# First columns of a modulation summed half on TensorE, deeper weight look-ahead in the mixer, and stage edges that keep their last weight blocks (hybrid macaron layer, Trainium2)

## The chip, the core and the metric

The kernel runs on one core of one Trainium2 chip. The metric is the device time of one execution in microseconds (us); lower is better. The kernel before took 2037.12 us, the median of three runs between 2032.08 and 2038.51 us.

## What is computed

One decoder layer on 256 tokens with a model width of 2048, all in float32. A condition vector `c` gives nine modulation vectors (shift, scale and gate of three parts). A SwiGLU network (FFN1, inner width 5632), a token mixer and a second SwiGLU network (FFN2) each read a normalised and modulated `x` and add their gated result to it:

```python
cond = silu(c)
mod = cond @ ada_w + ada_b                       # 2048 -> 9 * 2048
sh1, sc1, gt1, sh2, sc2, gt2, sh3, sc3, gt3 = split(mod, 9)
h = rmsnorm(x, g0) * (1 + sc1) + sh1
x = x + 0.5 * gt1 * ((silu(h @ w_gate1) * (h @ w_up1)) @ w_down1)
h = rmsnorm(x, g1) * (1 + sc2) + sh2
x = x + gt2 * (concat(forgetting_attention(h), gated_delta_rule(h)) @ w_out)
h = rmsnorm(x, g2) * (1 + sc3) + sh3
x = x + 0.5 * gt3 * ((silu(h @ w_gate2) * (h @ w_up2)) @ w_down2)
return rmsnorm(x, final_norm)
```

The mixer has eight attention heads with a forget gate and eight heads of a gated delta rule in chunks of 64 tokens; the latter needs a causal convolution of its inputs and the inverse of small triangular matrices.

## The kernel before

**Weights.** All large weights (353 MB, 5392 tiles) stream through once in a fixed list of blocks. A block is eight 128x128 tiles, 512 KB. `Stream.block` (L98) issues its DMA from SyncE (SP) into `wraw` (L103) and a ScalarE (ACT) cast to the reduced type, `whi` (L106); `Stream.low` (L109) has VectorE (DVE) write what the cast lost, `wlo` (L113). `wraw`, `whi` and `wlo` have three buffers each, and in some stages a fourth set for every fourth block. TensorE (PE) multiplies high by high, low by high and high by low (L576, L577, L579 in `products`). A *step* is four tiles against both halves of the tokens, six matmuls with 512 columns; two steps use up a block. In the mixer's input projections (`mm`, L516) a tile costs one matmul with 512 columns (L517) and one with 256 (L518).

**Order.** The program is emitted in order, and a scheduler fixes one instruction list per engine. Each engine works its list strictly in order, so a waiting instruction holds all behind it. `Stream.next` (L126) emits a block's load, cast and subtraction when its first tile is asked for; blocks in `W.early` (the mixer's) are emitted by `ahead` while the block before them is used, one block ahead. `tc.issue_after` pins an instruction behind another.

**Modulation.** Each of the 144 columns of `mod` needs 128 sums over 2048 numbers: a 1 MB load into a place of pool `adap` and one DVE reduction over 128x2048 (`ada_sum`, L286; two halves for the first two columns, L762). The table `RATE` says how many columns are emitted per block from a block number on; `W.quiet` stops them. The first 32 are the scale and shift columns of FFN1, two per `k`, since FFN1 needs `hs[k]`, its modulated input for `k` (128 of the 2048), `k` by `k`.

**Start.** `c` is loaded as a row (`crow`), spread to 128 partitions by matmuls (`pcs`, L226), passed through silu into `cs`; column 0 is loaded ahead of `x`; all squares of `x` are ACT's (L752), and DVE turns their sum into the row norm (`fv`, L771, to `frb`, L777). PE makes the transposes of `x` and some dummy matmuls (`warm_up`, L218). FFN1 then runs `k` in chunks 0-2, 2-8, 8-16 (`CHUNKS`); at the start of a chunk four groups of gate and up columns are run side by side for some `k` (`pgu`), afterwards one after the other. ACT copies the sums of chunk 0 to `acc` (L614).

**Edges.** The normalisation needs whole rows of `x`, so at the end of FFN1, of the mixer's output projection and of FFN2, `last_block` (L665) does the last ten steps for the first 128 tokens first and then for the others, so that the residual of the first half (`rs`, L540, `x`, L541), its square sum (`jq`, L384) and its inverse root (`nstd`, L396 to L401) are done meanwhile. The last six of these steps run first, and their weights are loaded a second time for the second half: three blocks per edge. Of the next stage, `modulate` (L425) transposes `xn` into `pxt` (L439) and scales it into `hs` (L451, L452) for `k` 0 and 1 of the first tokens ahead of the edge; that covers two `k` of the next stage for these tokens (12 matmuls `pv`, L857 to L859, in the mixer), until the second half's `xn` is there.

**Mixer.** Between the projections lie chains of small operations of the heads, cut into pieces by `tick` and `advance`. SP's list also holds the small DMAs of the triangular solve (`ld`, L1027; `x<-ld`, L1032; `xi<-x`, L1047), which wait for DVE.

## Time and profile before

| | |
|---|---|
| median of three runs | 2037.12 us |
| the profiled execution's own time | 2035.86 us |
| its span, first to last instruction | 2034.1 us |
| mean granted clock of PE | 0.991 |
| PE busy | 1987.4 us, 98% |
| DVE busy | 1494.7 us, 73% |
| ACT busy | 1001.4 us, 49% |
| moved by DMA | 528.92 MB, mean 260 GB/s |

A profile row of the timeline gives start, duration, engine, line of the kernel, what is written from what, the count, and in brackets the idle time of the engine before it with what ended it. A row of the waits gives who waited for whom, the sum, the count and the longest. Matmuls are pipelined: the time from the start of one to the start of the next is what counts, not a row's duration. FFN1 takes the span to about 771 us, the mixer to 1284 us, FFN2 to the end.

### The profile page before, as it was taken

To read this page: it belongs to the slowest core of one execution; us is meant where nothing else is said; L and a number is where in the kernel's file an instruction comes from. 1 tells how busy PE (TensorE), PEld (TensorE's weight loads), DVE (VectorE), ACT (ScalarE), POOL (GpSimd) and SP (SyncE) were. 2 spreads that over 40 slices of the span, in tenths; PEclk is the share of its full clock that TensorE was granted. 3 is DMA by queue.
4 is the path that set the end of the run, shared out by engine and by line. 5 is a ranking of instruction groups with operands and counts; after the bars stand their busy time and mean duration, and the time that the engine had idled before them with its cause. 6 is when DMAs were issued, how large, how long until landed. Compare 5 with 4: busy or idle time off the path is not lost.

```text
span 2034.1 us, 25528 instructions
## 1 busy us (share of the span) xinstructions
PE 1987.4 (98%) x9385; PEld 1648.0 (81%) x9385; DVE 1494.7 (73%) x2096; ACT 1001.4 (49%) x1451; POOL 2.6 (0%) x15
## 2 busy tenths in 40 slices
PE   8999999999999999998999999999999999999998
PEld 5788888888888887887888888788888888888886
DVE  6899999898787886689877887765566565455455
ACT  5544444343433456685657655644444333444444
POOL 0000000000000000000000000000000000000000
PEclk8999999999999999999999999999999999999999
DMA  8989898999788886564656577666666665555554
GB/s 323 349 326 349 314 344 333 354 387 375 298 331 338 325 304 243 185 214 155 209 205 220 187 259 267 219 218 239 249 243 231 239 238 196 187 192 189 207 195 167
DMA packets 134511, 528.92 MB, mean 260 GB/s; under 512 B 18489, under 2 KB 23785, under 8 KB 116081
## 3 DMA queue, kind: packets, MB, share of 16 engines
q1 hardware_dynamic: 134386, 527.29, 71.2%
q8 instruction: 73, 1.20, 0.2%
q14 instruction: 52, 0.43, 0.1%
HBM read 521.82 MB, written 5.41 MB: 259 GB/s over the span
## 4 chain that ended last, share of the span: by engine, by line
PE 91%; DVE 3%; DMA 3%; ACT 2%; issue 1%; ACTq 0%; DVEq 0%; SPq 0%
PE pgu L579 15%; PE pgu L577 15%; PE pgu L576 15%; PE pd L577 8%; PE pd L576 8%; PE pd L579 8%; PE pp L517 6%; PE pp L518 3%; DMA wraw<-in_w_dram 2%; DVE wlo L113 2%; PE pv L857 1%; PE pv L859 1%; PE pv L858 1%; PE po L577 1%; PE po L576 1%; PE po L579 1%
## 5 line engine op out<-in xcount | busy, mean ns | idle before, releaser
L106 ACT CAST whi<-wraw 128x1024 fp32r<-128x1024 f32 x683 | 714.8, 1051 | 833.7 <-PE pgu L577 280.3
L113 DVE TENSOR_TENSOR wlo<-wraw,whi 128x1024 fp32r<-128x1024 f32 x683 | 826.3, 1222 | 385.9 <-ACT whi L106 382.8
L576 PE MATMUL pgu<-whi,hs 128*128 128x512 f32 x1408 | 552.1, 394 | 14.8 <-ACT hs L411 6.5
L577 PE MATMUL pgu<-whi,hs 128*128 128x512 f32 x1408 | 550.5, 392 | 0.3
L579 PE MATMUL pgu<-wlo,hs 128*128 128x512 f32 x1408 | 438.0, 391 | 1.2 <-DVE wlo L113 1.2
L286 DVE CUSTOM_DVE_ANT_0 adat<-adat,cs,colt 128x2048 f32<-128x2048 f32 x140 | 328.7, 2348 | 41.4 <-DMA adat<-in_ada_dram 40.6
L576 PEld LDWEIGHTS pgu<-whi,hs 128*128 128x128 f32 x1408 | 266.0, 189 | 73.4 <-ACT hs L411 7.4
L579 PEld LDWEIGHTS pgu<-wlo,hs 128*128 128x128 f32 x1408 | 265.1, 189 | 58.4 <-DVE wlo L113 3.2
L577 PEld LDWEIGHTS pgu<-whi,hs 128*128 128x128 f32 x1408 | 266.2, 189 | 56.6 <-DVE hs L453 1.1
L576 PE MATMUL pd<-whi,hid 128*128 128x512 f32 x704 | 274.7, 390 | 0.0
L577 PE MATMUL pd<-whi,hid 128*128 128x512 f32 x704 | 273.9, 389 | 0.0
L517 PE MATMUL pp<-hs,whi 128*128 128x512 f32 x656 | 242.3, 405 | 8.7 <-ACT whi L106 8.7
L579 PE MATMUL pd<-wlo,hid 128*128 128x512 f32 x704 | 220.0, 389 | 0.0
L518 PE MATMUL pp<-hs,wlo 128*128 128x256 f32 x656 | 189.7, 290 | 1.3 <-DVE wlo L113 1.3
L576 PEld LDWEIGHTS pd<-whi,hid 128*128 128x128 f32 x704 | 132.2, 188 | 27.7 <-issue 0.2
L579 PEld LDWEIGHTS pd<-wlo,hid 128*128 128x128 f32 x704 | 132.2, 188 | 27.5
L577 PEld LDWEIGHTS pd<-whi,hid 128*128 128x128 f32 x704 | 132.2, 188 | 27.1
L517 PEld LDWEIGHTS pp<-hs,whi 128*128 128x128 f32 x656 | 124.8, 190 | 32.1 <-ACT whi L106 9.9
L518 PEld LDWEIGHTS pp<-hs,wlo 128*128 128x128 f32 x656 | 125.5, 191 | 2.5 <-DVE wlo L113 1.9
L857 PE MATMUL pv<-whi,hs 128*128 128x512 f32 x128 | 52.3, 411 | 0.5 <-ACT whi L106 0.3
L859 PE MATMUL pv<-wlo,hs 128*128 128x512 f32 x128 | 50.8, 398 | 0.0
L858 PE MATMUL pv<-whi,hs 128*128 128x512 f32 x128 | 50.6, 395 | 0.0
(313 smaller groups left out, 1369.9 us busy)
## 6 DMA issues: line engine op xcount, KB each, us to landing
wraw<-in_w_dram SPq DMA_DIRECT2D x683, 512.0 KB, 4.4
adat<-in_ada_dram SPq DMA_DIRECT2D x140, 1024.0 KB, 7.6
gtr<-gd SPq DMA_DIRECT2D x12, 256.0 KB, 6.2
rw<-rowd SPq DMA_DIRECT2D x24, 128.0 KB, 3.8
adaf<-in_ada_dram SPq DMA_DIRECT2D x4, 512.0 KB, 10.0
x<-in_xr_dram SPq DMA_DIRECT2D x4, 512.0 KB
adaf<-in_ada_dram SPq DMA_DIRECT2D x2, 1024.0 KB
xd<-x SPq DMA_DIRECT2D x4, 512.0 KB
```

Source lines behind the costliest of these rows:

```text
L106: self.cast = self.nc.scalar.copy(self.h, r).ins
L113: self.sub = self.nc.vector.tensor_tensor(self.l, r, self.h.bitcast(F32), ALU.subtract).ins
L286: V.tensor_tensor_reduce(t, t, cs, HALF.get(m, 1.0), L("adab", q, 1), ALU.mult, ALU.add, mod[:, q : q + 1])
L517: PE.matmul(ps, wt[0], act.rearrange("p a t -> p (a t)"), start=first, stop=False)
L518: PE.matmul(ps[:, :T], wt[1], act[:, 0], start=False, stop=last)
L576: PE.matmul(ps[t], hi_(t), wh, start=first, stop=False)
L577: PE.matmul(ps[t], lo_(t), wh, start=False, stop=False)
L579: PE.matmul(ps[t], hi_(t), wl, start=False, stop=last)
L857: PE.matmul(pv[m][t], hs[:, k, 0, sl], wh, start=(k == 0), stop=False)
L858: PE.matmul(pv[m][t], hs[:, k, 1, sl], wh, start=False, stop=False)
L859: PE.matmul(pv[m][t], hs[:, k, 0, sl], wl, start=False, stop=(k == KD - 1))
```

## The change

**Start.** `c` is loaded as a column, passed through silu (16 columns) and spread by DVE into diagonal tiles `dg`, which four float32 matmuls with a matrix of ones turn into `pcs`. `x` is loaded ahead of the columns; two of its four square sums go to DVE. The host packs the first four columns (two pairs) so that one 1 MB tile of a pair holds half of both columns for PE and the other tile holds the other half for DVE. `pe_sums` runs eight float32 matmuls 128x256 per pair into `pm`; `pair_sums` sums the other half on DVE (128x1024 per column) and takes the diagonal of `pm` with a 128x128 reduction per column. In chunk 0 three groups run side by side, not four. The first two rows `xn` are made before the columns. Columns 4 and 5 are loaded into places of the `hid` pool; `RATE` gives no column for blocks 0 to 2, one per block for 3 and 4.

**Stream.** `load` issues a DMA apart from `block`. For the mixer's blocks in `W.early`, the load is emitted three blocks ahead, cast and subtraction two.

**Edges.** `last_block` keeps the weights of all ten steps: six in tiles `hold`, four in `whi`, `wlo`. Nothing is loaded twice (nine blocks fewer in all). The next stage's first blocks are emitted during the last steps. `modulate` does `k` 0 to 3 of the first tokens ahead of the edge; the next stage starts with 18 matmuls `pv` (mixer) or eight steps of three matmuls (FFN2) on them. `W.quiet` is set in the output projection's column block 2, and `RATE` gives more columns from block 338 on.

On PE at the start of FFN1, before (`px` transposes of `x`, `pgu` the gate and up sums):

```order
L778 MATMUL nrow<-colt,frb 128x128 x2
L784 MATMUL px<-colt,x 128x128 x8
L576 MATMUL pgu<-whi,hs 128x512 x3
L577 MATMUL pgu<-whi,hs 128x512 x3
L576 MATMUL pgu<-whi,hs 128x512
L577 MATMUL pgu<-whi,hs 128x512
L579 MATMUL pgu<-wlo,hs 128x512 x4
L576 MATMUL pgu<-whi,hs 128x512
L577 MATMUL pgu<-whi,hs 128x512
```

and after:

```order
L614 MATMUL pgu<-whi,hs 128x512 x2
L615 MATMUL pgu<-whi,hs 128x512 x2
L614 MATMUL pgu<-whi,hs 128x512
L617 MATMUL pgu<-wlo,hs 128x512 x2
L615 MATMUL pgu<-whi,hs 128x512
L614 MATMUL pgu<-whi,hs 128x512
L615 MATMUL pgu<-whi,hs 128x512
L617 MATMUL pgu<-wlo,hs 128x512 x2
L839 MATMUL pm<-adat,cstt 128x256 x8
L614 MATMUL pgu<-whi,hs 128x512
```

The sums of the second pair of columns now stand in PE's list after the first twelve `pgu` matmuls.

On ACT at the same place, before (`acc` copies of chunk 0's sums):

```order
L106 CAST whi<-wraw 128x1024 x2
L410 ACTIVATE ht<-ht,mod 128x256
L411 CAST hs<-ht 128x256
L614 COPY acc<-pgu 128x512 x2
L106 CAST whi<-wraw 128x1024
L614 COPY acc<-pgu 128x512 x2
L106 CAST whi<-wraw 128x1024
L614 COPY acc<-pgu 128x512 x4
L106 CAST whi<-wraw 128x1024
```

and after:

```order
L126 CAST whi<-wraw 128x512 x2
L427 ACTIVATE hs<-xn,mod,g_277 128x256
L126 CAST whi<-wraw 128x1024 x2
L427 ACTIVATE hs<-xn,mod,g_343 128x256
L126 CAST whi<-wraw 128x1024
L652 COPY acc<-pgu 128x512 x8
L126 CAST whi<-wraw 128x1024 x3
L652 COPY acc<-pgu 128x512
```

Eight copies of `acc` now stand ahead of the cast of the fifth block; before, casts and copies alternated.

On DVE at the edge from the mixer to FFN2, before (`rs`, `x` the second half's residual, `adat` a column, `g` the scale that `hs` needs):

```order
L401 SCALAR_TENSOR_TENSOR nstd<-nya,nstd 128x1
L286 ISA adat,mod<-adat,cs,colt 128x2048
L286 ISA mod 128x1
L113 TENSOR_TENSOR wlo<-wraw,whi 128x1024
L286 ISA adat,mod<-adat,cs,colt 128x2048
L286 ISA mod 128x1
L540 TENSOR_TENSOR rs<-po,gtr 128x512
L422 SCALAR_TENSOR_TENSOR g_11397<-mod,colt 128x16
L541 TENSOR_TENSOR x<-x,rs 128x512
L452 TENSOR_SCALAR ht<-pxt,g_11397,mod 128x128
```

and after:

```order
L416 SCALAR_TENSOR_TENSOR nstd<-nya,nstd 128x1
L134 TENSOR_TENSOR wlo<-wraw,whi 128x1024 x2
L480 TENSOR_SCALAR ht<-pxt,g_11426,mod 128x128
L481 TENSOR_TENSOR hs<-ht,hs 128x128
L480 TENSOR_SCALAR ht<-pxt,g_11426,mod 128x128
L578 TENSOR_TENSOR rs<-po,gtr 128x512
L481 TENSOR_TENSOR hs<-ht,hs 128x128 x3
L579 TENSOR_TENSOR x<-x,rs 128x512
```

The two columns are gone from there, and the first tokens' `hs` work stands ahead of the second half's residual.

The core of the diff:

```diff
-RATE = ((0, 0.5), (24, 0.34), (56, 0.45), (68, 0.35), (112, 0.45), (168, 0.38), (266, 0.4), (282, 0.0), (300, 0.17), (412, 0.125))
+RATE = ((0, 0.0), (3, 1.0), (5, 0.5), (24, 0.34), (56, 0.45), (68, 0.35), (112, 0.45), (168, 0.38), (266, 0.4), (282, 0.0), (300, 0.17), (338, 0.25), (412, 0.125))
...
-N_WARM = (10, 5)
+N_WARM = (8, 6)
...
+    def load(self, b):
+
+        more = self.more and self.home is None and b % 4 == self.odd
+        r = (self.more[0] if more else self.raw).tile([P, WB * P], F32, name="wraw")
+        for q in self.pieces(b):
+            self.last = self.nc.sync.dma_start(r[:, q], self.w[b][:, q]).ins
+        return r, more
+
+    def pieces(self, b):
+
+        n = WB * P // 2
+        return (slice(0, n), slice(n, 2 * n)) if b == 0 else (slice(0, 2 * n),)
...
             self.now = b
-            if b + 1 in self.early:
-                self.ahead(b + 1)
+            if b + 3 in self.early:
+                self.loaded[b + 3] = self.load(b + 3)
+            for a in (b + 1, b + 2):
+                if a in self.early and a not in self.ready:
+                    self.ahead(a)
...
-                    n = 4 if len(chunks) > 1 else 3
+                    n = 4 if ci else 3
                     pb = {e: (psn(2 * i, "pgu"), psn(2 * i + 1, "pgu")) for i, e in enumerate(grp[:n])}
-                first = S_IN if need is h_need and pb else 0
-                wts = {(k, e): one(pb[e], *e, k, k0, k1, (0,)) for k in range(k0, k0 + first) for e in pb}
+                ahead = [(k, e) for k in range(k0, ks) for e in pb]
+                n = 8 if hq["todo"] else 0
+                wts = {(k, e): one(pb[e], *e, k, k0, k1, (0,)) for k, e in ahead[:n]}
                 for (k, e), wt in wts.items():
                     one(pb[e], *e, k, k0, k1, (1,), wt)
-                for k in range(k0 + first, ks):
-                    for e in pb:
-                        one(pb[e], *e, k, k0, k1)
+                for k, e in ahead[n:]:
+                    one(pb[e], *e, k, k0, k1)
...
-    def last_block(steps, weights, one, ps, m_gt, squares, begin):
-
-        twice, held = steps[-S_OUT : S_AGAIN - S_OUT], steps[S_AGAIN - S_OUT :]
+    def last_block(steps, weights, one, ps, m_gt, squares, begin, home):
+
         for f in steps[:-S_OUT]:
             one(f, weights(f), (0, 1), False)
-        for f in twice:
-            one(f, weights(f), (0,), False)
-        held = [(f, weights(f)) for f in held]
-        for f, wt in held:
-            one(f, wt, (0,), f == steps[-1])
+        W.home = home
+        held = []
+        for f in steps[-S_OUT:]:
+            if len(held) == S_HOME:
+                W.home = None
+            held.append((f, weights(f)))
+            one(f, held[-1][1], (0,), f == steps[-1])
+        held = held[S_HOME:] + held[:S_HOME]
         assert len(W.order) % WB == 0 and not W.ready
         b = len(W.order) // WB
-        n = S_AGAIN * 4 // WB
-        W.ahead(b)
+        if begin:
+            W.more, W.odd = None, (b + 3) % 4
+            W.ahead(b)
         residual(ps[0], 0, 3, m_gt, squares)
-        for i in range(1, n):
-            W.ahead(b + i)
-        for f, wt in held:
-            one(f, wt, (1,), False)
-        if squares != "final":
-            W.held = [yins[0]]
-            W.ahead(b + n, roots[0])
-        for f in twice:
-            if f == twice[-2] and begin:
+        W.held = [yins[0]]
+        for n, (f, wt) in enumerate(held):
+            if begin and n == 2:
+                W.ahead(b + 1, roots[0])
+            if begin and n == 4:
+                W.ahead(b + 2)
+            if begin and n == S_OUT - 2:
                 modulate(*begin)
-                hq["todo"].pop(0)[2]()
-            one(f, weights(f), (1,), f == twice[-1])
+                for _ in range(begin[-1]):
+                    h_pop()
+            one(f, wt, (1,), n == S_OUT - 1)
         residual(ps[1], 1, 3, m_gt, squares, yins[0])
-        if squares != "final":
-            W.held = [sums[1], yins[1]]
-
...
-    hold = None
-    for kind, i in (("c", 0), ("c", 1), ("c", 2), ("c", 3), ("x", 0), ("x", 1), ("x", 2), ("x", 3)):
...
-                t, q = divmod(i, 2)
-                hold = A.activation(junk, X(t, halves[q].start, D // 2), AF.Square, accum_out=s0[:, t, q : q + 1]).ins
+    bc_ = lambda a_, q, n: a_[:, q : q + n].unsqueeze(2).to_broadcast([P, n, P])
+    pcs = []
+    for q in range(4):
+        spread = V.tensor_tensor(dg[:, 4 * q : 4 * q + 4], ident.unsqueeze(1).to_broadcast([P, 4, P]), bc_(sc, 4 * q, 4), ALU.mult).ins
+        pcs.append(psn(q + 1, "pcs"))
+        in_order(pe, lambda: PE.matmul(pcs[q], one, dg[:, 4 * q : 4 * q + 4].rearrange("p a b -> p (a b)"), start=True, stop=True))
+    scb = cstt[:, : KD // 2 * P].rearrange("p (k a) -> p k a", a=P)
+    with tc.issue_after(spread):
+        V.tensor_copy(scb, bc_(sc, 0, KD // 2))
+    for q in range(4):
+        if q in (0, 2):
+            in_order(act, lambda: A.activation(junk, X(q // 2, 0, D // 2), AF.Square, accum_out=s0[:, q // 2, 0:1]))
+        else:
+            x1 = X(q // 2, D // 2, D // 2)
+            V.tensor_tensor_reduce(junk2, x1, x1, 1.0, 0.0, ALU.mult, ALU.add, s0[:, q // 2, 1:2])
+        if q:
+            for i in ((), (0, 1), (2,), (3,))[q]:
+                in_order(act, lambda: A.copy(cs[:, i * 512 : (i + 1) * 512], pcs[i]))
...
+    def pe_sums(pm, t, k0, k1):
+
+        for k in range(k0, k1):
+            in_order(pe, lambda: PE.matmul(pm[:, : 2 * P], scb[:, k], t[:, 2 * k * P : 2 * (k + 1) * P],
+                                           start=(k == 0), stop=(k == KD // 2 - 1)))
+
+    def pair_sums(pm, i, t):
+
+        part = tiny.tile([P, 2], F32, name="part")
+        for n in range(2):
+            m, j = ada_seq[i + n]
+            V.tensor_tensor_reduce(t[:, halves[n]], t[:, halves[n]], cs[:, D // 2 :], 1.0, L("adab", m * KD + j, 1), ALU.mult, ALU.add,
+                                   part[:, n : n + 1])
+        for n in range(2):
+            m, j = ada_seq[i + n]
+            junk3 = pt("junk3")[:, :P]
+            last = V.tensor_tensor_reduce(junk3, pm[:, n * P : (n + 1) * P], ident, 1.0, part[:, n : n + 1], ALU.mult, ALU.add,
+                                          mod[:, m * KD + j : m * KD + j + 1]).ins
+        return last
+
+    pm = pss("pm")
+    pe_sums(pm, first_ada[0], 0, KD // 4)
...
+        in_order(pe, lambda: PE.matmul(pr[:, t * P : (t + 1) * P], frb[:, t], ident, start=True, stop=True))
...
+    pe_sums(pm, first_ada[0], KD // 4, KD // 2)
+    zeros(N_WARM[1])
+    for j in range(2):
+        first_xn.append(tmp.tile([P, T], F32, name="xn", bufs=4))
+        V.tensor_tensor(first_xn[j], x_cols(j), first_row, ALU.mult)
+    pair_sums(pm, 0, first_ada[1])
...
+    def first_need(k, t):
+
+        calls.append(k)
+        if len(calls) == 1:
+            W.loaded[3] = W.load(3)
+            ada_room[:] = [ada_load(4 + n, hq["room"]()) for n in range(2)]
+        if len(calls) == 3:
+            room.append(psf("pm"))
+            pe[0] = tail[-1]
+            pe_sums(room[0], later[0], 0, KD // 2)
+        if calls.count(1) == 1 and k == 1:
+            with tc.issue_after(W.sub):
+                pair_sums(room[0], 2, later[1])
+            W.held = [modulate_one(1, gains(0, 1, 1, 1), mod[:, 1:2], first_row).ins]
+        ada_need(0, k)
...
-            first = S_IN if hq["todo"] else 0
+            todo = [(m, k) for k in range(KD) for m in mats]
+            n = 6 if hq["todo"] else 0
             held = []
-            for k in range(first):
-                for m in mats:
-                    held.append((m, k, W.next(m, k, 4 * grp, 4)))
-                    some(m, k, (0,), held[-1][2])
-            for m, k, wt in held:
+            for m, k in todo[:n]:
+                held.append((m, k, W.next(m, k, 4 * grp, 4)))
+                some(m, k, (0,), held[-1][2])
+            for i, (m, k, wt) in enumerate(held):
                 some(m, k, (1,), wt)
-            for k in range(first, KD):
-                for m in mats:
-                    some(m, k, (0, 1), W.next(m, k, 4 * grp, 4))
+                if i == 1:
+                    W.ahead(len(W.order) // WB)
+            if n:
+                W.early = set(range(len(W.order) // WB + 1, W.last_early))
+            for m, k in todo[n:]:
+                some(m, k, (0, 1), W.next(m, k, 4 * grp, 4))
...
+                last_block(list(range(KD)), weights, one, ps, 5, "mid", (2, 6, 7, 2),
+                           lambda: holdp.tile([P, 2 * WB * P], F32R, name="hold"))
...
+                if (b, i) == (2, KD // 2):
+                    W.quiet = True
...
+            h, p, q = D // 2, i // 2 * 2, i % 2
+            a[p].reshape(P, KD // 2, 2, P)[:, :, q] = aw[:h, o : o + P].reshape(KD // 2, P, P).transpose(1, 0, 2)
+            a[p + 1, :, q * h : q * h + h] = aw[h:, o : o + P].T
+            continue
```

239 lines of the change are left out of this document (128 added, 111 removed).

## Prediction

> **What bounds the kernel now.** I read the profile page first, then the list of waits of PE, then the timeline at the places that the waits name.
>
> ```profile
> PE 1987.4 (98%) x9385; PEld 1648.0 (81%) x9385; DVE 1494.7 (73%) x2096; ACT 1001.4 (49%) x1451; POOL 2.6 (0%) x15
> ...
> L106 ACT CAST whi<-wraw 128x1024 fp32r<-128x1024 f32 x683 | 714.8, 1051 | 833.7 <-PE pgu L577 280.3
> L113 DVE TENSOR_TENSOR wlo<-wraw,whi 128x1024 fp32r<-128x1024 f32 x683 | 826.3, 1222 | 385.9 <-ACT whi L106 382.8
> ```
>
> PE is busy for 98% of the span. The matmuls themselves are not changed in FFN1, mixer and FFN2, so the change can only win what PE waits, what it runs at a low clock, and something at the start; 47 us of the span are not busy, and the low clock hides inside the busy time. The waits, with sum, count and longest:
>
> ```profile
> PE pp L517 <- ACT whi L106: 8.7, 4, 2.9
> PE pgu L576 <- ACT hs L411: 6.5, 2, 3.9
> PE pgu L576 <- ACT hs L451: 4.0, 1, 4.0
> ...
> PE pxt L439 <- DVE xn L434: 2.3, 1, 2.3
> ...
> PE pp L518 <- DVE wlo L113: 1.3, 2, 1.1
> ```
>
> They lie at four places: `pp` in the mixer's projections, `hs` L411 in FFN1's first chunks, `hs` L451 at the edge mixer to FFN2, `xn` at the edge FFN1 to mixer. The diff touches all four.
>
> **Edge mixer to FFN2.** PE there, then DVE:
>
> ```profile
> 1283.59 0.40 PE L577 MATMUL po<-whi,oh 128*128 128x512 f32 x1
> 1283.82 0.40 PE L579 MATMUL po<-wlo,oh 128*128 128x512 f32 x1
> 1288.20 1.65 PE L576 MATMUL pgu<-whi,hs 128*128 128x512 f32 x3 [3.98 <-ACT hs L451]
> ...
> 1293.56 0.63 PE L579 MATMUL pgu<-wlo,hs 128*128 128x512 f32 x1
> 1293.99 0.63 PE L576 MATMUL pgu<-whi,hs 128*128 128x512 f32 x1
> ...
> 1294.82 0.40 PE L579 MATMUL pgu<-wlo,hs 128*128 128x512 f32 x1
> ```
> ```profile
> 1281.15 2.35 DVE L286 CUSTOM_DVE_ANT_0 adat<-adat,cs,colt 128x2048 f32<-128x2048 f32 x1
> ...
> 1284.56 2.35 DVE L286 CUSTOM_DVE_ANT_0 adat<-adat,cs,colt 128x2048 f32<-128x2048 f32 x1
> ...
> 1286.83 0.69 DVE L540 TENSOR_TENSOR rs<-po,gtr 128x512 f32<-128x512 f32 x1
> 1287.43 0.17 DVE L422 SCALAR_TENSOR_TENSOR g<-mod,colt 128x16 f32<-128x16 f32 x1
> ```
>
> PE steps 0.23 us from matmul to matmul before the edge. Then it starts nothing from 1283.82 to 1288.20, which loses 4.15 us, and afterwards steps 0.43 us until 1294.82: of these 6.6 us about half, 3.3, is lost to the clock. The edge costs 7.4 us. The cause is DVE: two columns of 2.35 us stand ahead of `g`, which `hs` needs, and ahead of the second half's `rs`. In the changed order both columns are gone and `modulate` does four pieces instead of one before the edge; the cover for the second half grows to 24 matmuls of 0.23, 5.4 us. What comes late next is the second half's `x`, behind three more `hs` pieces on DVE; I leave 0.5 us for it. **Gain 7**, between 5 (a wait of 2.4 without a clock loss stays) and 7.4. The columns move to blocks 338 and later; what hides them there is DVE's idle time, since PE never waits for `mod` but at an edge.
>
> **Edge FFN1 to mixer.** PE, then ACT and DVE:
>
> ```profile
> 774.80 0.73 PE L859 MATMUL pv<-wlo,hs 128*128 128x512 f32 x2
> 777.87 0.88 PE L439 MATMUL pxt<-colt,xn 128*128 128x128 f32 x6 [2.33 <-DVE xn L434]
> 778.86 2.08 PE L857 MATMUL pv<-whi,hs 128*128 128x512 f32 x4
> ...
> 782.44 0.55 PE L857 MATMUL pv<-whi,hs 128*128 128x512 f32 x1
> ```
> ```profile
> 774.53 1.05 ACT L106 CAST whi<-wraw 128x1024 fp32r<-128x1024 f32 x1 [0.41 <-DMA wraw<-in_w_dram]
> 778.35 0.46 ACT L451 ACTIVATE hs<-pxt,mod,g 128x128 fp32r<-128x128 f32 x1 [0.32 <-PE pxt L439]
> ...
> 776.33 1.22 DVE L113 TENSOR_TENSOR wlo<-wraw,whi 128x1024 fp32r<-128x1024 f32 x1
> ```
>
> From 774.80 to 778.86 PE does two `pv` (0.46) and six transposes (0.88): 2.7 us lost. Then it runs at half pace to 782.44, 3.6 us, of which 1.8 is lost. Together 4.5. In the way stood a cast that itself waited 0.41 us for its load, ahead of `nstd`, and a subtraction ahead of `xn`: 1.05 + 0.41 + 1.22 = 2.7, the whole wait. The change casts these blocks earlier, pins the next casts behind the root, and covers with 18 matmuls instead of 12, 1.4 us more. I leave 0.5 us. **Gain 4**, between 2.3 (the wait goes, something else holds the clock down) and 4.5. Not loading nine blocks twice gains nothing by itself: nine casts and subtractions (9 x 1.05, 9 x 1.22) leave engines that PE seldom waits for, and a DMA that is not late.
>
> **Mixer.** One of the four waits for `whi`, PE and ACT, and the stretches around it (PE, PEld, DVE, ACT, POOL busy with counts, clock, DMA share):
>
> ```profile
> 921.98 0.50 PE L517 MATMUL pp<-hs,whi 128*128 128x512 f32 x1 [2.82 <-ACT whi L106]
> ...
> 923.47 0.63 PE L517 MATMUL pp<-hs,whi 128*128 128x512 f32 x1
> 923.90 0.41 PE L518 MATMUL pp<-hs,wlo 128*128 128x256 f32 x1
> ```
> ```profile
> 919.11 1.28 ACT L986 ACT_TABLE_LOAD   x1
> ...
> 920.88 1.04 ACT L106 CAST whi<-wraw 128x1024 fp32r<-128x1024 f32 x1
> ```
> ```profile
> 850.00:900.00 50.00, 46.73 (x279) 40.63 (x279) 42.90 (x134) 46.76 (x111) 0.12 (x1) 0.97 0.59 190
> 900.00:950.00 50.00, 47.18 (x290) 41.85 (x289) 46.07 (x146) 32.45 (x72) 0.55 (x3) 0.97 0.60 198
> 950.00:1000.00 50.00, 44.91 (x287) 39.16 (x287) 46.32 (x133) 31.12 (x75) 0.00 (x0) 1.00 0.53 178
> ```
>
> ACT loads a table and does a head's work before it casts; the cast is one block ahead only, so such a delay falls on PE. The waits for `whi` and `wlo` are 8.7 + 1.3 = 10.0 us. Behind 921.98 PE steps 0.43 us for a 512-column matmul, and the clock of two of the stretches is 0.97: 2 x 0.03 x 50 = 3.0 us more. So 13 us are there to be had. With casts two blocks and loads three blocks ahead, a delay of a cast up to one more block's matmuls is covered; the four waits, 2.9 at most, are shorter than a block (8 tiles of 0.23 us and half of it, 2.8 us) or about one. But DVE is 92% busy from 900 to 1000, and the subtractions are its work; a quarter to a third of the waits I expect to come back as waits for `wlo`. **Gain 9**, between 0 and 18 (all of the 13, and 5 of the small gaps of the chains, which move too).
>
> The clock behaves here other than the Trainium skill says (TensorE: Matmul & The Clock Gate, Part 1): there the clock falls back to half only after an idle window of about 3.4 us, while here a wait of 2.82 us was enough. By the page's figure the mixer's waits would cost only themselves, the gain there would be about 7, and the sum below 20 instead of 22; I go by the rows.
>
> **Start.**
>
> ```profile
> 2.43 7.16 PE L226 MATMUL pcs<-crow,one 1*128 1x512 f32 x8 [2.43 <-DMA crow<-in_c_dram]
> 13.77 3.28 PE L784 MATMUL px<-colt,x 128*128 128x128 f32 x24
> 16.88 1.24 PE L218 MATMUL zp<-zw 128*128 128x512 bf16 x5
> ...
> 25.12 1.65 PE L576 MATMUL pgu<-whi,hs 128*128 128x512 f32 x3 [2.97 <-ACT hs L415]
> ...
> 35.03 0.63 PE L576 MATMUL pgu<-whi,hs 128*128 128x512 f32 x1 [2.66 <-ACT hs L411]
> ```
> ```profile
> 17.59 0.16 DVE L771 TENSOR_TENSOR fv<-s 128x2 f32<-128x2 f32 x1 [5.85 <-ACT junk L752]
> ...
> 21.77 1.28 DVE L762 CUSTOM_DVE_ANT_0 adaf<-adaf,cs,part 128x1024 f32<-128x1024 f32 x1
> ```
>
> DVE waited 5.85 us for ACT's last square. With `x` loaded first and two squares on DVE, I estimate `fv` 5 us earlier, most of that wait; two `xn` and two diagonals are new on the path behind it, so `hs[0]` comes 4.4 us earlier, PE's first `pgu` at about 20.7. Then twelve `pgu` at half pace (0.43, as after every such wait), 5.2 us, to 25.9. The second pair in `pm`: four float32 matmuls with 512 columns took 7.16 us right after an idle time, at half pace; eight with 256 columns have the same columns, so 7.2 at half pace and 3.6 at full. At full pace PE is through at 29.5; two diagonals, `g` and `hs` take some 1.7 (an estimate), so `hs[1]` is there at 31.2 instead of 35.03. But by then PE has done 18 matmuls instead of 24, 1.4 us less work: 2.4 us are won. Soon after, the cast of the fifth block stands behind eight copies of `acc` on ACT, which costs PE one cast at least (1.05), as it finishes the third group; before, such a stall lay behind fewer copies. DVE saves per column 2.35 - 1.28 and pays the diagonal, so the later columns come 1 to 2 us earlier. **Gain 2**, between -1.2 (the sums at half pace, 3.6 later, with 2.4 won) and 5.
>
> **The sum.** 7 + 4 + 9 + 2 = 22. Against the profiled execution's 2035.86 (its span plus 1.8) that is 2013.9, say 2014; the median of the three runs lies 1.3 above that execution. The tail keeps its order of work.
>
> **The rivals.**
> - *The mixer is DVE's* (0.22). Waits for `whi` become waits for `wlo` or for the chains, gain 0 there: 2023. For it: DVE 92% busy from 900 to 1000. Against: only 1.3 of the 10.0 us of waits are for `wlo` now.
> - *The start pays instead of gaining* (0.12). The second pair's sums run at half pace, 3.6 us more on PE: gain -1.2, total 2017. For it: 25.12 is at half pace now. Against: twelve matmuls, 5.2 us, go before them. The Trainium skill has a reason for it (the same page, Part 4): transposes in PE's transpose mode don't count as activity for the clock, and 32 of them stand ahead in the start. The trace doesn't bear that out: five matmuls right behind 24 `px` took 1.24 us, 0.25 each, full pace.
> - *More of the mixer goes* (0.10): the small gaps too, gain 18, total 2005.
> - *The edges and the look-ahead change little* (0.06): another instruction takes the place of each one removed (three more `hs` pieces ahead of the residual), total about 2034.
> - *Slower* (0.06): ACT is held by the casts ahead. Three `whi` buffers mean that a cast two blocks ahead must wait for PE to finish the block before the one in use; ACT's list is in order, so the heads' work waits behind it, and PE for the heads. From 850 to 1000 ACT is busy 110.3 of 150 us and PE uses about 43 blocks (2.8 us each and the chains between): 39.7 / 43 = 0.92 us of waiting per cast is free. Beyond 1.25 us it eats all other gains (43 x 0.33 = 14 against 7 + 4 + 2); at half a block, 1.4 us, it costs 43 x 0.48 = 20.6 - 13 = 7.6 us net: 2044. Against: ACT can only be early where it has nothing else to do.
>
> **How the numbers follow.** My forecast has 0.44. The range goes from 2000 (all gains at their upper ends, 4.5 + 7.4 + 18 + 5 = 35) to 2030 (the lower ends, 2.3 + 5 + 0 - 1.2 = 6), which leaves out the last two rivals. A measurement tells 0.3% from no change, 6.1 us. Faster by more than that: 0.86, within 0.08, slower 0.06.
>
> **What would show it.** In the profile after: no wait over 1 us and a 0.23 step at both edges; no wait of `pp` for `whi` over 1 us between 850 and 1000, clock 1.00 there; first `pgu` near 20.7, `hs[1]` near 31. I am wrong if `pp` waits for `wlo` or small matmuls for DVE by 10 us or more, if the step after an edge is 0.43, or if ACT's casts show long waits for PE while chains are late.

## The result, and the profile after

The changed kernel takes 2026.02 us, the median of five runs (2023.51 to 2027.09). Five runs of the kernel before, on the same chip, have the median 2037.12 (2032.08 to 2038.91). The ratio is 0.9947, 95% interval 0.9931 to 0.9964: 11.1 us or 0.53% faster, half of the 22 that were forecast. The profiled execution took 2023.51 us, with a span of 2021.7 us and a mean granted clock of 0.993. It is the fastest of the five, so it lies 12.4 below the profiled one of before.

The page's row of the engines, after:

```profile
PE 1986.8 (98%) x9416; PEld 1647.6 (81%) x9416; DVE 1486.4 (74%) x2109; ACT 994.5 (49%) x1447; POOL 2.6 (0%) x15
```

PE is as busy as before, in a span 12.4 us shorter. The list of PE's waits after (sum, count, longest):

```profile
PE pp L556 <- DVE wlo L134: 6.1, 2, 4.2
PE pgu L614 <- ACT hs L427: 3.5, 2, 2.2
PE pgu L614 <- ACT whi L126: 3.2, 2, 1.9
PE pgu L617 <- DVE wlo L134: 3.2, 4, 1.1
PE pgu L614 <- DVE acc L655: 2.5, 1, 2.5
...
PE pp L555 <- ACT whi L126: 0.5, 1, 0.5
```

The 4.0 us for `hs` at the edge to FFN2 and the 2.3 for `xn` are gone, and the mixer's wait for casts fell from 8.7 to 0.5. But its wait for subtractions rose from 1.3 to 6.1, and the start has waits that it did not have before.

To see where the 12.4 us come from I took, from the timelines of both profiled executions, the start of the same matmul at each border of a stage (matmuls are counted from 0):

| stage, us | before | after | difference |
|---|---|---|---|
| start to the 600th `pgu` | 175.38 | 176.08 | +0.7 |
| on to FFN1's last `pd` | 596.05 | 596.21 | +0.2 |
| edge 1: on to the 100th `pv` | 31.24 | 26.54 | -4.7 |
| mixer: on to the last `po` | 481.16 | 478.56 | -2.6 |
| edge 2: on to FFN2's 100th `pgu` | 33.90 | 27.48 | -6.4 |
| on to FFN2's last `pd`, and the end | 716.35 | 716.85 | +0.5 |

The edges alone give 11.1. Edge 1 on PE after:

```profile
772.30 0.39 PE L617 MATMUL pd<-hold,hid 128*128 128x512 f32 x1
772.53 0.40 PE L960 MATMUL pv<-whi,hs 128*128 128x512 f32 x1
...
776.80 0.76 PE L467 MATMUL pxt<-colt,xn 128*128 128x128 f32 x4
...
777.78 0.73 PE L960 MATMUL pv<-whi,hs 128*128 128x512 f32 x2 [0.23 <-ACT hs L479]
```

From the last `pd` to the first `pv` it is 0.23 us, and the 18 matmuls on the first tokens cover the second half's `xn`: the wait of 2.33 is 0.23. Edge 2:

```profile
1277.40 0.39 PE L617 MATMUL po<-hold,oh 128*128 128x512 f32 x1
1277.63 0.40 PE L614 MATMUL pgu<-whi,hs 128*128 128x512 f32 x1
...
1284.02 0.50 PE L614 MATMUL pgu<-whi,hs 128*128 128x512 f32 x1 [1.36 <-ACT whi L126]
1284.36 0.39 PE L615 MATMUL pgu<-whi,hs 128*128 128x512 f32 x1
1284.59 0.39 PE L614 MATMUL pgu<-whi,hs 128*128 128x512 f32 x1
```

The 3.98 us are gone. One wait of 1.36 us for a cast remains, and PE goes on at 0.23 us a matmul behind it.

### The profile page after: what moved, and what is told of

Its sections match the earlier page's. It is cut to its first block, busy times and chain, and to the rows that moved or that the text cites. A ratio compares the mean times of both kernels' runs of the same rounds, so it can differ in the third digit from the quotient of the medians.

```text
span 2021.7 us, 25585 instructions
## 1 busy us (share of the span) xinstructions
PE 1986.8 (98%) x9416; PEld 1647.6 (81%) x9416; DVE 1486.4 (74%) x2109; ACT 994.5 (49%) x1447; POOL 2.6 (0%) x15
## 4 chain that ended last, share of the span: by engine, by line
PE 92%; DVE 4%; ACT 2%; DMA 1%; issue 1%; SPq 0%; ACTq 0%; DVEq 0%
PE pgu L617 15%; PE pgu L614 15%; PE pgu L615 15%; PE pd L617 8%; PE pd L615 8%; PE pd L614 8%; PE pp L555 6%; PE pp L556 3%; PE pv L962 1%; PE pv L961 1%; PE pv L960 1%; DVE wlo L134 1%; PE po L614 1%; PE po L615 1%; PE po L617 1%; PE pz L635 1%
## 5 line engine op out<-in xcount | busy, mean ns | idle before, releaser
L126 ACT CAST whi<-wraw 128x1024 fp32r<-128x1024 f32 (+1 forms) x666 | 697.3, 1051 | 800.0 <-PE pgu L615 329.9
L134 DVE TENSOR_TENSOR wlo<-wraw,whi 128x1024 fp32r<-128x1024 f32 (+1 forms) x666 | 804.5, 1220 | 388.8 <-ACT whi L126 386.4
L614 PE MATMUL pd<-whi,hid 128*128 128x512 f32 x680 | 265.1, 390 | 0.0
L615 PE MATMUL pd<-whi,hid 128*128 128x512 f32 x680 | 264.6, 389 | 0.0
L617 PE MATMUL pd<-wlo,hid 128*128 128x512 f32 x680 | 210.7, 389 | 0.0
L614 PEld LDWEIGHTS pd<-whi,hid 128*128 128x128 f32 x680 | 127.7, 188 | 26.7
L617 PEld LDWEIGHTS pd<-wlo,hid 128*128 128x128 f32 x680 | 127.6, 188 | 26.7 <-DVE wlo L134 0.3
L615 PEld LDWEIGHTS pd<-whi,hid 128*128 128x128 f32 x680 | 127.7, 188 | 26.3
```

The lines of the kernel that those rows point to most:

```text
L126: self.cast = self.nc.scalar.copy(self.h[:, q], r[:, q]).ins
L134: self.sub = self.nc.vector.tensor_tensor(self.l[:, q], r[:, q], self.h[:, q].bitcast(F32), ALU.subtract).ins
L614: PE.matmul(ps[t], hi_(t), wh, start=first, stop=False)
L615: PE.matmul(ps[t], lo_(t), wh, start=False, stop=False)
L617: tail[:] = [PE.matmul(ps[t], hi_(t), wl, start=False, stop=last).ins]
```

## The experiments

The stage times in this section come from the timelines of each run's profiled execution, as in the table above. Every ratio is to the kernel before, run beside the build on the same chip, with its 95% interval. The chips differ between experiments, so builds are compared by these ratios or by stage times, not by their medians; a stage time is that of one execution. Lines of code are the changed kernel's.

### The mixer: look-ahead, DVE's work, DVE's order

In the mixer the wait that replaced the casts is this one. PE, ACT and DVE there, after:

```profile
952.58 0.58 PE L556 MATMUL pp<-hs,wlo 128*128 128x256 f32 x1 [4.16 <-DVE wlo L134]
952.95 0.63 PE L555 MATMUL pp<-hs,whi 128*128 128x512 f32 x1
```
```profile
942.90 1.04 ACT L126 CAST whi<-wraw 128x1024 fp32r<-128x1024 f32 x1
...
945.27 1.04 ACT L126 CAST whi<-wraw 128x1024 fp32r<-128x1024 f32 x1
```
```profile
938.05 1.21 DVE L134 TENSOR_TENSOR wlo<-wraw,whi 128x1024 fp32r<-128x1024 f32 x1
939.18 0.24 DVE L1147 TENSOR_TENSOR x<-x 64x96 f32<-64x96 f32 x1
...
951.31 1.21 DVE L134 TENSOR_TENSOR wlo<-wraw,whi 128x1024 fp32r<-128x1024 f32 x1
```

The two casts end at 943.9 and 946.3. DVE does no subtraction from 939.2 to 951.3, because its list has the triangular solve there (`x<-x`, L1147 and L1148) with the heads' small operations between its steps.

**One block ahead again** (`m_one`): casts and loads of the early blocks as before, all else as changed.

```diff
-            if b + 3 in self.early:
-                self.loaded[b + 3] = self.load(b + 3)
-            for a in (b + 1, b + 2):
-                if a in self.early and a not in self.ready:
-                    self.ahead(a)
+            if b + 1 in self.early and b + 1 not in self.ready:
+                self.ahead(b + 1)
```

> The changed kernel with the mixer's look-ahead undone: load, cast and subtraction of a block one block ahead, as before. From the traces, the mixer's stretch (100th pv matmul to the last po matmul) took 481.2 us before and 478.6 us after. Theory DVE (the look-ahead only moves waits from the casts to the subtractions, because VectorE's list in order is full there): the stretch goes back to about 481 to 482, the total is 2.5 to 3.5 us above the changed kernel's. Rival OTHER (the look-ahead did win its 9 us, and another part of the change, the moved columns or the pins, took 6 of them): the stretch is 487 or more, the total 8 to 10 us above.

2025.19 us, ratio 0.9954 (0.9938 to 0.9969), which can't be told from the changed kernel (0.9947). The mixer's stretch is 481.0 against 478.6, as theory DVE had it, and waits for casts are back:

```profile
PE pp L552 <- ACT whi L126: 4.2, 2, 2.2
```

So here the deeper look-ahead does what it says to the casts, and the time barely shows it. It doesn't do so in every build: in `start_old2` below, also two blocks ahead, `pp` waits 5.3 us for casts.

**Less work for DVE** (`lo_copy`): the early blocks' subtraction becomes a copy.

```diff
             for q in self.pieces(b):
+                if b in self.early:
+                    self.sub = self.nc.vector.tensor_copy(self.l[:, q], r[:, q]).ins
+                    continue
```

> The changed kernel, but for the mixer's blocks emitted ahead VectorE copies the raw weights where it should subtract; the low part of these weights is therefore not computed. The copy should be about half as long as the 1.22 us subtraction. Theory DVE: with some 70 us less work in VectorE's list, the waits for wlo (6.1 us) and part of the chains' waits go: the mixer's stretch falls from 478.6 to 470 or less. Rival LOADS (SyncE's list, blocked by the solve's small DMAs, brings the blocks late): the stretch stays within 2 us of 478.6, with waits for casts or loads in place of those for wlo.

2024.21 us, ratio 0.9946 (0.9928 to 0.9964); the mixer's stretch is 480.9, not shorter. PE's waits for `wlo` are gone, and others stand in their place:

```profile
PE pft L1362 <- issue: 3.4, 1, 3.4
PE pp L558 <- ACT whi L126: 3.2, 3, 2.0
PE pk L1110 <- DVE Ln L1123: 2.0, 2, 1.3
```

From 850 to 1000 DVE is busy 119.9 us by the windows, against 134.9 with the subtraction. With 11% of its work there taken away nothing is won, so the sum of DVE's work does not set the mixer's time.

**Another order on DVE** (`solve_3`): the solve yields more often, so that other work gets between its steps.

```diff
-                if i % 4 == 3:
-                    yield 1.0
+                if i % 2 == 1:
+                    yield 2.0
```

> The changed kernel with the solve's chain of 30 small VectorE operations emitted in eight pieces with gaps of 2.0 instead of four with gaps of 1.0; no operation is added or left out. In the changed kernel's list some 55 operations, the second solve among them, stand between two subtractions, and PE waits 4.2 us for the next wlo at 948 us. Theory LIST (what is left in the mixer is the order of VectorE's list, not the sum of its work): that wait goes, the mixer's stretch falls from 478.6 to 473 to 475, total 3 to 6 us below the changed kernel's. Rival CHAIN (the heads' serial chains set the mixer, a wait removed comes back at the next place): the stretch stays within 2 us of 478.6.

2023.91 us, ratio 0.9948 (0.9936 to 0.9961). The list of waits:

```profile
PE pp L556 <- DVE wlo L134: 4.2, 4, 1.9
```

The wait of 4.16 is down to 1.9 at most, and the stretch is 479.5, longer than the changed kernel's 478.6. The order made that wait, but taking it away gave nothing.

**No solve** (`no_solve`): the 30 operations of L1147 and L1148 per half are left out.

```diff
-                V.tensor_tensor(pv, Xv[:, :, :m], L_[:, 16 * i : 16 * i + m].unsqueeze(1).to_broadcast([64, 16, m]), ALU.mult)
-                V.tensor_reduce(Xv[:, :, i], pv, mybir.AxisListType.X, ALU.add)
```

> The changed kernel with the solve's 30 VectorE operations per half left out (the inverse of the small triangles is replaced by the identity; the DMAs and all that follows stay). Theory CHAIN (the heads' serial chains and VectorE's list in them set the mixer between 850 and 1000 us, of which the solve is the longest piece, about 10 us per half): the mixer's stretch falls from 478.6 to 473 or less. Rival ACT (ScalarE, 94% busy from 850 to 900 us, and its table loads hold the casts and the heads): the stretch stays within 2 us of 478.6.

2020.67 us, ratio 0.9932 (0.9917 to 0.9947); the stretch is 473.9, 4.7 shorter than the changed kernel's, while those of all other builds lie between 477.9 and 482.3. The waits for `wlo` are 1.6 us. DVE is busy 127.4 us from 850 to 1000 here, more than in `lo_copy` (119.9), where nothing was won. So what the solve costs isn't the time that DVE is busy. I put it down to the chain of a head, where one step waits for the last; that is argued, since no run shortens the chain and keeps its place in DVE's list.

### The start: its own parts, and what sets its pace

After, the first `pgu` come early, and `pm` runs at full pace:

```profile
19.80 0.73 PE L614 MATMUL pgu<-whi,hs 128*128 128x512 f32 x2 [2.17 <-ACT hs L427]
...
22.69 3.62 PE L839 MATMUL pm<-adat,cstt 128*128 128x256 f32 x16
25.96 0.58 PE L614 MATMUL pgu<-whi,hs 128*128 128x512 f32 x1
...
28.99 0.73 PE L614 MATMUL pgu<-whi,hs 128*128 128x512 f32 x2 [1.31 <-ACT hs L427]
...
38.28 0.50 PE L614 MATMUL pgu<-whi,hs 128*128 128x512 f32 x1 [1.88 <-ACT whi L126]
```

Yet the table has the 600th `pgu` no earlier than before. The lead, 5.3 us at the first `pgu` (19.80 against 25.12), is 1.3 us at the 100th (52.8 against 54.1) and 0.7 at the 250th (88.8 against 89.5). From there to the 400th the changed kernel takes 41.9 us and the kernel before 40.6. PE there, and DVE:

```profile
107.32 0.53 PE L614 MATMUL pgu<-whi,hs 128*128 128x512 f32 x1 [2.48 <-DVE acc L655]
```
```profile
103.12 2.34 DVE L301 CUSTOM_DVE_ANT_0 adat<-adat,cs,colt 128x2048 f32<-128x2048 f32 x1
105.39 2.48 DVE L655 TENSOR_TENSOR acc<-pgu,acc 128x512 f32<-128x512 f32 x4
```

A column's sum stands ahead of the additions to `acc`, and PE has no free `pgu` until they are done. Half pace follows, up to 114.48 us.

**The old start** (`start_old`): the code of before for the start, the rest as changed. The core of the edit:

```diff
-N_FIRST = 2
+N_FIRST = 4
...
-N_WARM = (8, 6)
+N_WARM = (10, 5)
```

> The changed kernel with the start of the kernel before (row of c, whole columns on VectorE, four groups in the first chunk, the old rate of columns); stream, mixer and edges as changed. Theory PACE (the columns set the pace of FFN1's first 110 us, so that a start that is 4 us ahead at the second k ends nowhere): the last pd matmul of FFN1 at 771 to 772 us against 772.3 in the changed kernel and 771.4 in the kernel before; total the same within 1.5 us. Rival START (the new start did win 2 us and the end of FFN1 came late for another reason): the last pd at 774 or later, total 2 us or more above the changed kernel.

2039.88 us, ratio 1.003 (1.002 to 1.004): slower than before. FFN1's last `pd`, at 777.3, and the total are where rival START had them, but not for its reason: the start itself is shorter (174.4 us to the 600th `pgu`), and it is FFN1's and FFN2's long stretches that grew, 596.2 to 602.8 and 706.9 to 714.7 us, with the same work in them. The old start has other tiles, and so all pools behind them lie elsewhere. The constant `FILL`, the width of an unused tile ahead of the pools, is 112 in the kernel before and 96 in the changed one; a step of 16 moves the pools by 64 bytes in each partition.

**The old start, and the old place** (`start_old2`):

```diff
-FILL = 96
+FILL = 112
```

> start_old once more, with the filler tile of 112 numbers per partition that the kernel before has (FILL) instead of 96, so that the tiles behind it stand where they stand in the other kernels. In start_old FFN1 from its 600th matmul on took 602.8 us and FFN2 714.7, against 596.2 and 706.9 in every other run, with pd matmuls 0.231 us apart instead of 0.227. Theory PLACE (that is the place of the tiles in memory alone): 596 and 707 again, and the total falls by 14 us to 2024 to 2027, which is what the edges and the mixer give without the new start. Rival OLD (it comes with the old start): 602 and 714 stay, total 2038 or more.

2023.62 us, ratio 0.9946 (0.9933 to 0.996). The long stretches are 596.8 and 707.1 again. The place explains it: 13.6 of the 14.4 us between these two traces lie in the two stretches. By the ratios the new start is worth nothing that can be told (0.9947 with it, 0.9946 without, intervals of some 3 us to either side).

**The place alone** (`fill112`): the changed kernel with the same one line, 96 to 112.

> The changed kernel with FILL 112 instead of 96: nothing else moves than the places of the tiles behind the filler, by 64 bytes. Theory PLACE: FFN1's main part 6 to 7 us and FFN2 7 to 8 us longer, pd matmuls 0.231 apart, total 2036 to 2042, no gain over the kernel before. Rival OLD: total within 2 us of the changed kernel's 2026.

2043.51 us, ratio 1.0046 (1.0033 to 1.006): for 64 bytes, the trace is 19 us longer than the changed kernel's, 17 of them in the two long stretches. The same matmuls in the changed kernel, then here:

```profile
740.10 0.39 PE L615 MATMUL pd<-whi,hid 128*128 128x512 f32 x1
...
741.46 0.39 PE L615 MATMUL pd<-whi,hid 128*128 128x512 f32 x1
```
```profile
740.49 0.40 PE L615 MATMUL pd<-whi,hid 128*128 128x512 f32 x1
...
741.89 0.40 PE L615 MATMUL pd<-whi,hid 128*128 128x512 f32 x1
```

Between the two rows lie six steps in each: 0.227 us a step in one, 0.233 in the other.

**The other side** (`fill80`): 96 to 80.

> The changed kernel with FILL 80 instead of 96: the tiles behind the filler 64 bytes lower. fill112 made each pd matmul 0.233 instead of 0.227 us apart and the kernel 17 us slower. Theory PLACE-STEP (a place is right or wrong by its offset within some larger stride): slow as fill112, 2035 or more, or equal at 2026; both say that 96 belongs to the change as much as its code. A place better than 96 would show as matmuls less than 0.227 apart and a total under 2020.

2040.41 us, ratio 1.0024 (1.0015 to 1.0033), with 0.230 us a step (the median of the `pd` matmuls). So both neighbours are slow, and builds can only be compared where their long stretches agree. From here on each experiment is read with those stretches beside it.

**Half of a column's sum** (`cols_sum`): DVE adds up half of each of columns 4 to 31; they are still loaded whole.

```diff
+            n = D // 2 if m < 2 else D
-            V.tensor_tensor_reduce(t, t, cs, HALF.get(m, 1.0), L("adab", q, 1), ALU.mult, ALU.add, mod[:, q : q + 1])
+            V.tensor_tensor_reduce(t[:, :n], t[:, :n], cs[:, :n], HALF.get(m, 1.0), L("adab", q, 1), ALU.mult, ALU.add, mod[:, q : q + 1])
```

> The changed kernel, but VectorE sums only half of each of the modulation columns 4 to 31 of FFN1 (the loads are whole; the other half of these sums is left out): 28 x 1.07 = 30 us less work in VectorE's list in the first 110 us. Theory PACE-DVE (VectorE's list is what paces FFN1's first chunks): the waits at 97 to 111 us go, the last pd of FFN1 falls from 772.3 to 766 or less. Rival PACE-DMA (the loads pace it, 95% of the DMA engines' time is used there, and casts wait for loads): less than 2 us change.

2020.21 us, ratio 0.9929 (0.9913 to 0.9945). The 200th to the 600th `pgu` take 93.7 us instead of 98.6, and FFN1's last `pd` is at 769.9: a gain of 2.4 us there, between what the two theories had.

**Half of a column's load too** (`cols_load`): the same, and the other half isn't loaded either.

```diff
-            nc.sync.dma_start(t, adaw[i])
+            n = D // 2 if i < 2 * KD else D
+            nc.sync.dma_start(t[:, :n], adaw[i][:, :n])
```

> As cols_sum (half of the sums of columns 4 to 31 left out), and the half that is not summed is not loaded either: 14 MB less through the DMA queues in the first 110 us. In cols_sum the stretch from FFN1's 200th to its 600th matmul fell from 98.5 to 93.7 us. Theory PACE-DVE: VectorE's list alone paced it, no more than 1 us further (92.7 or more). Rival BOTH (the loads pace it as soon as VectorE doesn't): 91 us or less there, the ideal at 0.227 us a matmul being 90.8, and less in the first 200 matmuls too.

2009.9 us, ratio 0.9879 (0.9866 to 0.9893). Now these 400 matmuls take 90.7 us, which is 400 x 0.227: PE waits for nothing. The windows from 50 to 100 us (PE, PEld, DVE, ACT, POOL, clock, DMA share, GB/s), the changed kernel, then this one:

```profile
50.00:100.00 50.00, 47.64 (x206) 38.28 (x207) 45.41 (x50) 28.33 (x40) 0.00 (x0) 1.00 0.95 351
```
```profile
50.00:100.00 50.00, 50.00 (x222) 41.44 (x221) 42.51 (x59) 28.90 (x38) 0.00 (x0) 1.00 0.91 311
```

And what ACT's casts wait for from 50 to 150 us:

```profile
ACT whi L126 <- DMA wraw<-in_w_dram: 22.1, 12, 3.0
ACT whi L126 <- PE pgu L617: 41.2, 27, 1.9
```

The first row is the changed kernel's, in which the loads are late; in the second, of `cols_load`, the loads are early and the casts wait for PE. The 600th `pgu` comes at 172.9 us without half of the sums and at 163.0 without half of the loads too, instead of 176.1: the loads of the first 32 columns, and next to them their sums, pace this part of FFN1. A lead of PE at 30 us is therefore given back: it only makes PE ask sooner for what is not there. In the kernel before, the loads are as dense:

```profile
50.00:100.00 50.00, 47.57 (x207) 38.22 (x206) 43.99 (x49) 26.92 (x38) 0.00 (x0) 1.00 0.94 347
```

**Another cut of the chunks**, to ask for columns later: `chunks7` and `chunks6`.

```diff
-CHUNKS = (0, 2, 8, 16)
+CHUNKS = (0, 2, 7, 16)
```

> The changed kernel with FFN1's chunks of k at 0-2, 2-7, 7-16 instead of 0-2, 2-8, 8-16: two columns less are needed by about the 22nd block, and the same sums are made. In cols_load the start ended 16 us earlier with 14 MB less to load, so the loads pace it: by block 24 all of 16 columns and 24 blocks, 28 MB, and x are needed, 80 to 90 us at 350 GB/s. Theory PACE-DMA (what is needed by when decides): FFN1's 600th matmul at 171 to 174 us instead of 175 to 178, total 2 to 4 us below the changed kernel's. Rival SUM (all bytes up to the 600th matmul count, whatever their order): within 1.5 us of 176.5.

2034.51 us, ratio 0.9996 (0.9982 to 1.0009). The 600th `pgu` is at 176.8, as rival SUM had it, and the rest of FFN1 is 10.8 us longer, in a profiled execution (2038.66) near the upper end of twelve from 2028.08 to 2039.57.

```diff
-CHUNKS = (0, 2, 8, 16)
-LEAD = (2, 5, 5)
+CHUNKS = (0, 2, 6, 16)
+LEAD = (2, 4, 5)
```

with 0.42 columns per block from block 5 on.

> As chunks7 with chunks 0-2, 2-6, 6-16, four k side by side in the second, and columns emitted at 0.42 per block instead of 0.5 from block 5 to 24: 12 columns by about block 20. Theory PACE-DMA: 169 to 173 us at the 600th matmul, total 3 to 6 us below the changed kernel's. Rival SUM: within 1.5 us of 176.5. A third way: the third chunk's columns come late instead, with waits for hs between 110 and 160 us.

2047.3 us, ratio 1.0065 (1.005 to 1.0079). The 600th `pgu` comes 6 us sooner, at 169.8, and the rest of FFN1 takes 25 us more, with waits for `whi` and `hs` up to 230 us. In this build PACE-DMA was right about the 600th `pgu` and wrong about the total: a later date for the columns moved the waits behind it, where they cost more.

### The edges

**The columns back at the edge** (`edge_cols`): the later columns' rate and the quiet ahead of FFN2 taken out.

```diff
-RATE = (..., (300, 0.17), (338, 0.25), (412, 0.125))
+RATE = (..., (300, 0.17), (412, 0.125))
...
-                if (b, i) == (2, KD // 2):
-                    W.quiet = True
```

> The changed kernel without the two edits that keep the modulation columns away from the edge mixer to FFN2 (the rate from block 338 on, and the stop in the output projection's second to last column block). Theory COLUMNS (the columns in VectorE's list were the edge's wait, the longer cover is the smaller half): the stretch from the last po matmul to FFN2's 100th pgu, 33.9 us before and 27.5 after, goes back to 31 or more, with a wait for hs of 2 us or more and a 0.43 us step; total 3 to 6 us above the changed kernel's 2026. Rival COVER (the 24 matmuls of cover are enough also with the columns there): 28.5 or less.

2028.39 us, ratio 0.9967 (0.9955 to 0.9979). Edge 2 takes 31.5 us instead of 27.5; every other stage is within 1 us. PE, then DVE:

```profile
1277.46 0.40 PE L617 MATMUL po<-hold,oh 128*128 128x512 f32 x1
1280.59 0.96 PE L614 MATMUL pgu<-whi,hs 128*128 128x512 f32 x3 [2.74 <-ACT hs L479]
...
1282.82 0.63 PE L615 MATMUL pgu<-whi,hs 128*128 128x512 f32 x1
1283.24 0.63 PE L617 MATMUL pgu<-wlo,hs 128*128 128x512 f32 x1
```
```profile
1275.27 2.35 DVE L301 CUSTOM_DVE_ANT_0 adat<-adat,cs,colt 128x2048 f32<-128x2048 f32 x1 [1.45 <-DMA adat<-in_ada_dram]
...
1279.82 0.17 DVE L443 SCALAR_TENSOR_TENSOR g<-mod,colt 128x16 f32<-128x16 f32 x1
```

A column that itself waited for its load stands ahead of `g`, PE waits 2.74 us and then steps 0.42 us. Of the 6.4 us at this edge, 4.1 are due to the columns' new place. The other 2.3, and the 4.7 at edge 1, no run takes apart.

**What of all this is worth keeping?** Two builds. `both` has the old start (with `FILL` 112) and the solve that yields more often.

> The edges and the look-ahead of the change with the start of the kernel before (start_old2) and the solve in eight pieces (solve_3). Theory EDGES (the gain is the edges', the new start gives nothing or costs 2 us, the mixer is set by its chains): total 2021 to 2025, not slower than the changed kernel. Rival START (start_old2 was a lucky build, the new start is worth its 2 us): 2026 or more.

2023.96 us, ratio 0.9945 (0.9931 to 0.9959): together they are worth nothing over the changed kernel.

`edges_only` is the kernel before with the new edges and the columns' new rate: old start, `FILL` 112, one block ahead, the edits shown above for `start_old2` and `m_one` together.

> The change's edges alone: start of the kernel before, load and cast one block ahead in the mixer, FILL 112. Theory EDGES: the two edge stretches keep their 4.7 and 6.5 us, the mixer is 481 to 483, the total 9 to 12 us below the kernel before, so 2023 to 2027, which is the whole gain of the change. Rival SHARED (the edges need the deeper look-ahead, whose first blocks they emit): an edge stretch 2 us or more longer, or a total of 2029 or more.

2018.89 us (2017.41 to 2019.78), ratio 0.9918 (0.9904 to 0.9931): 16.8 below before, and by the ratios some 6 below the changed kernel, with intervals that touch; the best version of all that compute the whole layer. Its edges take 26.6 and 27.2 us, as expected. The total is 4 us below the lower end of what was expected: of the 16 us between its trace and that of before, 11.4 lie at the edges, and 3.3 in the mixer and 2.0 ahead of the 600th `pgu`, where its code is that of before. That part is luck as far as these runs show. Its list of PE's waits from 760 to 1300 us shows that the mixer still waits for casts:

```profile
PE pp L555 <- ACT whi L126: 3.4, 3, 2.6
...
PE pp L556 <- DVE wlo L134: 1.5, 2, 1.1
```

Its mixer takes 477.9 us all the same. It differs from `start_old2` by the look-ahead alone, and there one block ahead is 5.7 us faster by the ratios and 4.4 by the stretches (482.3 against 477.9); with the new start the same edit (`m_one`) was 1.4 us slower by the ratios, within the noise, and its stretch 2.4 longer.

## Why the prediction was half right

**Right: both edges.** Gain 4 at edge 1 was 4.7, gain 7 at edge 2 was 6.4; the cause named for edge 2, columns ahead of `g` on DVE, is shown by `edge_cols` for 4.1 us; the rest, and the cause named for edge 1, fit the traces but were not tested alone. The 0.5 us left for the second half's `x` became 1.36 us for a cast, without a loss of clock. Together 11.1 in the traces, as much as the medians differ by.

**Wrong: "Gain 9" in the mixer.** That "a delay of a cast up to one more block's matmuls is covered" held in this build: 8.7 us of waits became 0.5. The step that failed is the next one, that only "a quarter to a third of the waits" come back as waits for `wlo`, and with it the sum, which counted the other waits and 3.0 us of lost clock as time won. Of these 8.2 us 4.8, more than half, came back as waits for `wlo`, and the clock took most of the rest; its sign "clock 1.00 there" failed as well. The windows of the changed kernel, to be held against those of before:

```profile
850.00:900.00 50.00, 46.24 (x276) 39.61 (x275) 41.70 (x144) 47.01 (x111) 0.12 (x1) 0.97 0.56 181
900.00:950.00 50.00, 48.42 (x303) 41.92 (x301) 47.67 (x159) 34.06 (x78) 0.54 (x3) 1.00 0.64 204
950.00:1000.00 50.00, 47.02 (x291) 41.90 (x292) 45.57 (x111) 31.92 (x72) 0.00 (x0) 0.93 0.55 180
```

What falls short of clock 1.00 is 0.03 + 0.07 of 50 us, 5.0 us, where it was 3.0 (from rounded rows). Waits 3.4 less and clock 2.0 more leave 1.4 us; the stretch is 2.6 shorter. I had read the waits as a store of time to be emptied. I now read them as the place where the longest chain happens to touch PE: with casts early the subtraction is late (`m_one` against the changed kernel), with the subtraction cheap the heads' own steps are late (`lo_copy`), with the solve spread out nothing is won (`solve_3`), and only a chain that is shorter shortens the stretch (`no_solve`). Over the builds that keep the whole mixer the stretch lies between 477.9 and 482.3 us in no stable relation to the look-ahead: two ahead 478.6, 479.5, 482.3 and 478.4, one ahead 481.2, 481.0 and 477.9. A gain of 9 is excluded; the sign of what is left is open, since any edit reorders the lists of all engines there.

**Wrong: "Gain 2" at the start.** Its steps held or came out better but for one: the first `pgu` at 19.80 (forecast 20.7), no half pace behind it, `pm` in 3.3 us (3.6), `hs[1]` at 28.99 (31.2), only the fifth block's stall was longer, 1.88 (1.05), with 3.4 us at half pace behind it. What failed is that a lead there is kept. Neither the sum nor a rival asked what FFN1 would be short of next: the columns' loads and sums (`cols_load`, `cols_sum`). In six builds with the new start the 600th `pgu` lies at 175.2 to 178.4, mean 176.8; in five with the old one at 171.6 to 175.4, mean 173.7. So the lead is lost and some 3 us with it in the traces, while the ratios of the changed kernel and `start_old2` show no difference. The record shows where: from the 250th to the 400th `pgu` the six take 41.8 to 42.4 us and the five 38.7 to 40.6. In all six PE waits 2.5 us there for `acc`, behind a column's sum on DVE, and goes on at half pace for 6.8 us; with the old start the wait for `acc` is 0.3 us or none, and three of the five lose no clock there. Why DVE's list comes out in that order isn't settled.

**The rivals.** "The mixer is DVE's" came nearest with 2023 and had the sign of the waits right, but its cause, DVE's total work, fell with `lo_copy`. "Slower", by ACT held behind casts ahead, didn't happen: from 850 to 1000 ACT's casts wait 13.4 us for PE, against 12.1 before, and the mixer's stretch is not longer. The start's rival on half-pace sums fell with `pm`'s 3.3 us. The reason given for it was that transposes don't count as activity for the clock. The five matmuls at 0.25 us that the prediction held against it were no test, since the clock had gone to full at 14.77 us, 1.0 us into the `px` and behind ten dummy matmuls. Another stretch speaks against that reason: in the changed kernel PE does nothing but transposes from 8.44 to 12.06 us (`px`), and the granted clock stays 1.00 through and behind them. The Trainium skill (TensorE: Matmul & The Clock Gate, Part 4) says that transposes in the transpose mode don't count as PE being busy in the same way; the trace doesn't say whether these ran in that mode. The 0.5 us at the end were not forecast and not looked into.

What I would have needed: for each wait that is removed, the next late item in the lists of all engines that feed PE. Both could be seen in the trace of before: the solve in DVE's list, and DMA busy for 94% of the time from 50 to 100 us.

## What to carry to other kernels

A wait in a chain of in-order engines shows where the longest path touches PE; removing it can be worth only the distance to the next late item, so look for that item (a list that holds it up, a load that isn't there) before taking the wait's length as a gain. A lead won ahead of a stretch that is paced by loads is given back within it; ask first what paces that stretch. Test each part of a change alone and with the tiles at the same places: here the edges alone beat the whole change (0.9918 against 0.9947), and 64 bytes of shift outweighed everything.
